# Loading, memory and order in the front part of a transformer block on one Trainium2 core

## The chip, the core and the metric

The kernel runs on one core of a Trainium2 chip. The core has a matrix engine (TensorE, "PE" in the profile), a vector engine (VectorE, DVE), a scalar engine for activations (ScalarE, ACT), a general engine (GpSimd, POOL) and a sync engine (SyncE, SP), which here issues every transfer between the chip's DRAM and the on-chip memories. Matmul results land in PSUM, a small memory of eight banks; everything else on chip lies in SBUF, 128 partitions wide. Each engine works through its own queue in order and waits on semaphores. The metric is the device time of one execution in microseconds; lower is better.

## The reference, cut to what matters

The reference is one hybrid block on x of 1024 positions by 1024 channels, all in float32. Its input projection `w_in` feeds three mixers, and the changed part of the kernel is what stands in front of their attention:

```
hn = rms_norm(x, norm_mix_g)
u  = hn @ w_in            # columns: MLA 672 | fox q,k,v,f 1544 | z, xBC, dt | gates
c_q (384), c_kv (256), k_rope (32) = split(u_mla)
q  = rms_norm(c_q) @ w_uq      # 8 heads of 96
kv = rms_norm(c_kv) @ w_ukv    # 8 heads of 64 + 64
q, k = rope_tail(rms_norm(q)), rope_tail(rms_norm(k))    # rotation by positions
fox: q, k = rms_norm per head of 64; log_f = log_sigmoid(f + b_f), cumulated
ssm: dt = softplus(dt_raw + dt_bias); cumulated dt*A; y * silu(z)
```

Behind it come two attentions (MLA and "fox", the latter with forget gates), a state-space scan, the gated merge, and a gated MLP with a short convolution.

## The kernel before, in words

All matmuls keep float32 accuracy by splitting: each operand is written as a high part (rounded to the matmul's format, `split`, L142, on ScalarE) and the remainder (L143, on VectorE). `mm3` (L167) then issues three matmuls per 128-deep slice: high by high, high by low, low by high. Activations must also be transposed on TensorE before they can be the stationary operand; a transposed group goes through PSUM and is split from there.

The tokens are eight tiles of 128. The front part has three stages.

*Latents* (L351 to L405). For each token tile: load x, `norm_tile` (square and sum on ScalarE, an inverse root by eleven or so short VectorE instructions, the scaled row, then eight transposes and the split into `hnh`, `hnl`); two products with the latent columns of `w_in`, 384 columns (`cq`) and 312 columns (`ckv`: 288 latent columns, 8 forget-gate and 16 dt columns); their normalisation into `cn`; five transposes and the split into `ch[t]`, `cl[t]`. The weights are loaded by `wsplit` through five buffers `raw`: sixteen loads of one 128-row slice each, and sixteen tiny ones for the 8 and 16 columns. `rope_and_columns` builds the cosine and sine tables with a long chain of GpSimd instructions, loads the positions so that each partition gets eight single numbers, and turns parameter rows into columns by transposes.

*Heads and values* (L422 to L519). For each tile: `q` (18 matmuls of 384 columns) and `kv` (12 of 512) from the latents, head norms, rotation on GpSimd, 16 transposes into four PSUM groups, split, and four kinds of stores to DRAM (`q_h`, `q_l`, `k_h`, `k_l`). The fox values (`fxv`, 24 matmuls of 256 columns per tile) come in two halves behind the loop over tiles, each half with weights of its own (`load_cols`) in the same buffers.

*Wide projections* (L615 to L683). Four blocks of 512 columns (z first half, fox q, fox k, z second half), eight tiles each, 24 matmuls of 512 columns per tile (`fx`). `load512` loads and splits a block's weights at its beginning, through the two `wr` buffers. The q and k units are normalised per head, transposed at once, split and stored; `gate_sums` computes the cumulated forget gates and decays between the first two blocks. `down_sums` prepares sums of the MLP's down weights on GpSimd, through four buffers `t4`.

[...] Only inside a `tc.manual_schedule(engines=...)` does the named engine keep the written order. Before the change there was none in the front part; from attention on, TensorE (and in attention VectorE too) was already in written order.

PSUM in the front: four buffers `mm` and two `mv` for results, and two `tp` for transposes, eight banks in all. SBUF is a stack of pools: a new pool may lie where a closed one lay, and its tiles wait for the last use of what was there.

Of the kernel before, what the change touches and what calls it, by code (L numbers as in the profile page):

```python
# [11 lines left out]
F32 = mybir.dt.float32  # L12
# [30 lines left out]
def block_kernel(ctx: ExitStack, tc: tile.TileContext, x, positions, norm_mix_g, w_in, b_gate,  # L43
# [132 lines left out]
    def norm_tile(pool, tag, spool, psp, xt, gbc, h, l, t, ptag):  # L176
# [12 lines left out]
        if wide:  # L189
            A.activation(xn, xg, AF.Copy, scale=r)  # L190
        else:
            V.scalar_tensor_tensor(out=xn, in0=xt, scalar=r, in1=gbc, op0=ALU.mult, op1=ALU.mult)
        half, c0 = t // 4, (t % 4) * P
# [29 lines left out]
    def rope_and_columns(rp):  # L223
# [18 lines left out]
        pos_i = rp.tile([P, NT], I32, name="pos_i", tag="pos_i", bufs=1)  # L242
        SY.dma_start(pos_i, positions.rearrange("o (t p) -> p (o t)", p=P))
        pos_f = rp.tile([P, NT], F32, name="pos_f", tag="pos_f", bufs=1)
        tc.keep_in_program_order(G.tensor_copy(pos_f, pos_i))
# [49 lines left out]
        pr = rp.tile([84, P], F32, name="pr_g", tag="pr", bufs=1)  # L295
        SY.dma_start(pr[0:24, :], b_gate.rearrange("o (r p) -> (o r) p", p=P))
        SY.dma_start(pr[24:72, :], ssm_conv_w.rearrange("o k (r p) -> (o k r) p", p=P))
        SY.dma_start(pr[72:84, :], ssm_conv_b.rearrange("o (r p) -> (o r) p", p=P))
        pt = psp.tile([P, 84], F32, name="pcp", tag="tp", bufs=2)
        T.transpose(pt, pr, ident[0:84, 0:84])  # L300
        A.activation(pc_g, pt, AF.Copy, scale=0.5)
        for dst, srcs in ((pc_f1, (ffn_conv_w[:, 0, :], ffn_conv_w[:, 1, :])),
                          (pc_f2, (ffn_conv_w[:, 2, :], ffn_conv_b))):
            pr = rp.tile([88, P], F32, name=uid("pr_f"), tag="pr", bufs=1)
            for i, s in enumerate(srcs):
                SY.dma_start(pr[44 * i:44 * i + 44, :], s.rearrange("o (r p) -> (o r) p", p=P))
            pt = psp.tile([P, 88], F32, name=uid("pcp"), tag="tp", bufs=2)
            T.transpose(pt, pr, ident[0:88, 0:88])
            A.activation(dst, pt, AF.Copy)
        pr = rp.tile([NK, P], F32, name="pr_n", tag="prn", bufs=1)  # L310
        SY.dma_start(pr, ssm_norm_g.rearrange("o (r p) -> (o r) p", p=P))
        pt = psp.tile([P, NK], F32, name="pcn", tag="tp", bufs=2)
        T.transpose(pt, pr, ident[0:NK, 0:NK])
        A.activation(pc_n, pt, AF.Copy)
# [11 lines left out]
    pmla = ExitStack()  # L326
# [5 lines left out]
    ch = [chp.tile([P, 5, P], F32R, name=f"ch{t}", tag=f"ch{t}") for t in range(NT)]  # L332
    cl = [chp.tile([P, 5, P], F32R, name=f"cl{t}", tag=f"cl{t}") for t in range(NT)]

    with ExitStack() as p0:
# [6 lines left out]
        def wsplit(pool, tag, shape, pieces):  # L342
            h = pool.tile(shape, F32R, name=tag + "h", tag=tag + "h", bufs=1)
            l = pool.tile(shape, F32R, name=tag + "l", tag=tag + "l", bufs=1)
            for k, c0, c1, srcs in pieces:
                raw = mp.tile([P, 384], F32, name=uid("raw"), tag="raw", bufs=5)
                for a, b, src in srcs:
                    SY.dma_start(raw[:, a:b], src)
# [7 lines left out]

        load_x(0)
        gmix = bcast(norm_mix_g[0], D, "gmix", ap_)
        norm_tile(ap_, "xn", mp, psp, xts[0], gmix, hnh, hnl, 0, "tp")
        load_x(1)  # L360
        w1h, w1l = wsplit(mp, "w1", [P, NK, 384], [
            (k, 0, 384, [(0, 384, w_inv[:, k, C_Q:C_Q + 384])]) for k in range(NK)])
        w2h, w2l = wsplit(mp, "w2", [P, NK, 312], [
            (k, 0, 312, [(0, 288, w_inv[:, k, C_KV:C_KV + 288]),
                         (288, 296, w_inv[:, k, C_F:C_F + 8]),
                         (296, 312, w_inv[:, k, C_DT:C_DT + 16])]) for k in range(NK)])
# [1339 lines left out]
```

## Time and profile before

| what | us |
|---|---|
| median of three runs | 2099.43 (2095.68 to 2100.97) |
| profiled execution, own time | 2103.04 |
| its span in the trace | 2101.3 |
| TensorE busy in the span | 2030.5 (97%) |
| VectorE, ScalarE, GpSimd busy | 1400.8, 953.7, 619.9 |
| span up to the last `fx` matmul | about 428 |

"Busy" is the time in which an engine had at least one instruction under way. Matmuls are pipelined, so a busy TensorE isn't one at its peak; "PEclk" is the share of its full clock that the chip granted. A wait is listed with the instruction that ended it.

### The profile page before, as it was taken

What the parts mean: (1) busy time and instruction counts of PE and PEld (TensorE: products, weight loads), DVE (VectorE), ACT (ScalarE), POOL (GpSimd) and SP (SyncE); (2) the same over time, 40 slices, a digit from 0 to 9 for tenths busy, and PEclk for the clock granted to TensorE, in tenths of its full rate; (3) what the DMA queues carried; (4) which work ended last, traced back from release to release, by engine and by line L of the source; (5) the groups of instructions that cost most, each with busy time, mean ns of one, the idle gap of its engine ahead of it and who ended that gap; (6) DMA issues with size and microseconds to landing.
All of it is one profiled execution on the core that took longest, in us unless ns stands there. A gap on an engine that the chain in (4) does not pass through costs nothing.

```text
span 2101.3 us, 29138 instructions
## 1 busy us (share of the span) xinstructions
PE 2030.5 (97%) x10265; PEld 1685.4 (80%) x10265; DVE 1400.8 (67%) x2595; ACT 953.7 (45%) x1739; POOL 619.9 (30%) x606
## 2 busy tenths in 40 slices
PE   7999898999999999999999999999989999999999
PEld 6898787788888888787777888888778888887887
DVE  5687467456667776666887346556887666765664
ACT  5555222146565666554554323223444544444432
POOL 2454122322222222220000031001454455431755
PEclk9999999999999999999999999999999999999999
DMA  5057767754443554324342665441122222229675
GB/s 172 25 178 223 230 211 238 241 154 115 124 130 95 135 150 125 95 87 138 112 136 77 200 190 191 150 141 51 61 95 85 81 80 90 81 88 350 238 222 194
DMA packets 276650, 303.62 MB, mean 144 GB/s; under 512 B 19308, under 2 KB 209784, under 8 KB 276504
## 3 DMA queue, kind: packets, MB, share of 16 engines
q1 hardware_dynamic: 276504, 301.76, 46.6%
q8 instruction: 81, 1.33, 0.3%
q14 instruction: 65, 0.53, 0.1%
HBM read 209.03 MB, written 92.67 MB: 144 GB/s over the span
## 4 chain that ended last, share of the span: by engine, by line
PE 78%; DMA 8%; DVE 6%; POOL 3%; issue 2%; ACT 2%; SPq 1%; DVEq 0%; ACTq 0%; POOLq 0%
PE mm L796 18%; PE dn L1653 9%; PE ybr L167 8%; PE ua L1322 5%; PE uc L1322 4%; PE ud L1322 4%; PE wo L1368 4%; PE s L886 4%; PE fx L167 4%; PE tp L955 2%; PE ub L1322 2%; DMA att_d<-o 2%; PE fxv L167 1%; PE o L926 1%; PE kv L167 1%
## 5 line engine op out<-in xcount | busy, mean ns | idle before, releaser
L796 PE MATMUL mm<-hnh,wh 128*128 128x512 f32 x576 | 250.6, 435 | 0.0
L796 PE MATMUL mm<-hnh,wl 128*128 128x512 f32 x576 | 227.0, 394 | 0.0
L796 PE MATMUL mm<-hnl,wh 128*128 128x512 f32 x576 | 225.6, 392 | 0.0
L908 POOL TENSOR_SCALAR pm<-pm,rs 128x128 f32<-128x128 f32 (+7 forms) x128 | 108.0, 846 | 349.9 <-DVE rs L907 316.7
L1653 PE MATMUL dn<-dr,dr 128*128 128x512 f32 x592 | 182.2, 389 | 0.0
L961 DVE TENSOR_TENSOR ptl<-tp,pth 128x512 fp32r<-128x512 f32 (+1 forms) x160 | 101.3, 633 | 86.4 <-ACT pth L960 85.6
L891 DVE TENSOR_REDUCE nmx<-s 128x1 f32<-128x128 f32 (+2 forms) x192 | 105.6, 550 | 56.1 <-PE s L889 44.5
L901 ACT ACTIVATE pm<-s,nmx 128x128 f32<-128x128 f32 (+2 forms) x192 | 109.7, 576 | 55.5 <-DVE nmx L898 38.1
L1653 PEld LDWEIGHTS dn<-dr,dr 128*128 128x128 f32 x592 | 111.1, 188 | 23.0
L796 PEld LDWEIGHTS mm<-hnh,wl 128*128 128x128 f32 x576 | 108.3, 188 | 24.8
L796 PEld LDWEIGHTS mm<-hnl,wh 128*128 128x128 f32 x576 | 109.2, 190 | 18.5 <-issue 4.1
L796 PEld LDWEIGHTS mm<-hnh,wh 128*128 128x128 f32 x576 | 109.0, 189 | 17.8 <-issue 4.1
L960 ACT ACTIVATE pth<-tp 128x512 fp32r<-128x512 f32 (+1 forms) x160 | 88.2, 551 | 70.2 <-PE tp L955 69.4
L886 PE MATMUL s<-qk,qk 96*128 96x384 f32 (+5 forms) x480 | 117.6, 350 | 1.0 <-ACT pm L901 0.9
L1238 POOL TENSOR_TENSOR mg<-mg,gl 128x512 f32<-128x512 f32 x16 | 24.9, 1560 | 315.2 <-DVE gl L1235 315.1
L1653 PE MATMUL dn<-dr 128*128 128x512 f32 x296 | 115.3, 390 | 0.3 <-ACT dX L1657 0.3
L142 ACT ACTIVATE wh<-wr 128x1024 fp32r<-128x1024 f32 (+1 forms) x47 | 43.0, 914 | 145.1 <-PE ua L1322 60.8
L167 PE MATMUL fx<-w5h,hnh 128*128 128x512 f32 x256 | 101.8, 402 | 7.1 <-ACT w5h L142 7.1
L143 DVE TENSOR_TENSOR dr<-dr,dr 128x1024 fp32r<-128x1024 f32 x52 | 73.4, 1411 | 52.5 <-ACT dr L142 47.5
L167 PE MATMUL fx<-w5h,hnl 128*128 128x512 f32 x256 | 101.3, 397 | 0.0
L167 PE MATMUL fx<-w5l,hnh 128*128 128x512 f32 x256 | 101.0, 396 | 0.0
L167 PE MATMUL ybr<-al,wh 128*128 128x512 f32 x256 | 99.2, 390 | 0.0
(469 smaller groups left out, 5822.8 us busy)
## 6 DMA issues: line engine op xcount, KB each, us to landing
dr<-act_d SPq DMA_DIRECT2D x99, 256.0 KB
wr<-in_ffn_w_up_dram SPq DMA_DIRECT2D x47, 512.0 KB
wr<-in_w_in_dram SPq DMA_DIRECT2D x36, 512.0 KB
g_d<-t SPq DMA_DIRECT2D x24, 512.0 KB
gl<-g_d SPq DMA_DIRECT2D x24, 512.0 KB
ws<-in_ffn_w_down_dram SPq DMA_DIRECT2D x22, 512.0 KB
wsum_d<-ws SPq DMA_DIRECT2D x22, 512.0 KB
act_d<-fa SPq DMA_DIRECT2D x22, 512.0 KB
```

Source lines behind the costliest of these rows:

```text
L143: return i, le.tensor_sub(l, src, f32(h))
L167: T.matmul(ps, a(k), b(k), start=(i == 0), stop=(i == n - 1))
L796: T.matmul(ps, a[:, k, :], b[half][:, k, :], start=(k == 0 and i == 0), stop=(k == NK - 1 and i == 2))
L886: T.matmul(ps[:, :w], q_[:, qs], k_[:, a:a + w], start=i_ == 0, stop=not last and i_ == len(o.passes) - 1)
L891: later(c + 0.1, lambda ps=ps, ci=ci, a=a, b=b: V.reduce_max(nmx[:, ci:ci + 1], ps[:, :b - a], axis=AX, negate=True))
L901: pss[ci][1][0] = later(c + 0.9 + 0.1 * ci, lambda ci=ci, a=a, b=b: A.activation(p_[:, a:b], pss[ci][0][:, :b - a], AF.Exp, bias=nb, accum ...
L908: G.tensor_scalar(p_[:, 0:n * P], p_[:, 0:n * P], rs[:, 3:4], 0.0, op0=ALU.mult, op1=ALU.add)
L960: later(c + 0.05, lambda th=th, pt=pt, off=off: A.activation(th[:, :off], pt[:, :off], AF.Copy))
L961: pl[0] = later(c + 0.6, lambda th=th, tl=tl, pt=pt, off=off: V.tensor_sub(tl[:, :off], pt[:, :off], f32(th[:, :off])))
L1322: T.matmul(ps, a, b, start=first and n == 0, stop=n == 11, skip_group_check=not first)
L1368: T.matmul(p, a, b, start=k == 0 and i == 0, stop=k == NK - 1 and i == 2)
L1653: T.matmul(ps[m], a[:, ts_], b[:, 512:], start=first_ and j == 0 and q == 0, stop=j == NFH - 1 and q == 2, skip_group_check=not first_)
```

## The change

Loads. The latent columns are loaded as pieces of up to three 128-row slices by 672 columns (`load_cols2`, `split_cols2`), the first six slices into memory that belongs to the later tiles `chB` and `clB`, the rest through small buffers. The 8 and 16 tiny columns come by two loads for all slices at once. Positions are loaded as 8 rows of 128, cast, transposed on TensorE and copied; the parameter rows get buffers of their own and are loaded together.

Memory. `ch` and `cl` become four tiles of four tokens each. The second half of the value weights is split into the tiles of the first four tokens (`chA`, `clA`) once these are used. The raw columns of the first z block get a pool of their own (`zr`), the later blocks use the `wh` and `wl` buffers of the later fill work, the `t4` buffers also hold `Fh` and `Fl`, and `fsh`, `fsl` get two buffers each.

Order. `norm_tile` is cut into `norm_chain` and `norm_turn`, the latent norm from its transposes. TensorE keeps the written order from the third tile's turning to the end of the values; in the wide stage TensorE, VectorE and ScalarE do. The values move into the loop over tiles, head turnings come two tiles late, fox turnings two units late, weight splits are spread over the odd units of the block before, and `gate_sums` becomes a generator in seven steps.

```diff
+        def load_cols2(k0, k1, c0=0, c1=672):
+            if k1 <= 6:
+                raw = wraw[k0 // 3][:, k0 % 3:k0 % 3 + k1 - k0, :]
...
+            SY.dma_start(raw, w_inv[:, k0:k1, C_Q + c0:C_Q + c1])
...
+        chain(0)
+        for part in parts:
+            split_cols2(*part)
+        split(w2h[:, :, 288:312], w2l[:, :, 288:312], rfd)
+        turn(0)
...
+        pe_front = tc.manual_schedule(engines={mybir.EngineType.PE})
+        pe_front.__enter__()
+        turn(2)
+        next(rot)
+        for t in range(1, NT):
+            if t + 4 < NT:
+                load_x(t + 4)
+            if t + 2 < NT:
+                chain(t + 2)
+            p1 = latent(t, 0)
+            latent_turn(t - 1)
+            p2 = latent(t, 1)
+            if t + 2 < NT:
+                turn(t + 2)
+            latent_norm(t, p1, p2)
...
+    def heads_turn(t, qn, kn):
+        for src, col, dsts in ((qn, gq_col, (q_h, q_l)), (kn, gk_col, (k_h, k_l))):
+            for g in range(2):
+                pt = tps()
+                for j in range(4):
+                    T.transpose(pt[:96, j, :], src[:, 4 * g + j, :], ident)
+                sh = mp.tile([96, 4, P], F32R, name=uid("sh"), tag="sh")
+                sl = mp.tile([96, 4, P], F32R, name=uid("sl"), tag="sl")
+                A.activation(sh, pt[:96, :, :], AF.Copy, scale=col)
+                V.scalar_tensor_tensor(out=sl, in0=pt[:96, :, :], scalar=col, in1=f32(sh),
+                                       op0=ALU.mult, op1=ALU.subtract)
...
         for t in range(NT):
+            if t > 1:
+                heads_turn(*heads.pop(0))
+            if t == 4:
+                vcols.append(load_v(*(f32r_halves(four(n)) for n in ("chA", "clA")), 256))
...
+            heads.append((t, qn, kn))
+            if t == 0:
+                latent_turn(NT - 1)
+            values(t, 0, fv_tile(False))
+            if t > 4:
+                values(t - 5, 256, fv_tile(False))
+        pup.close()
+        zrp = pup.enter_context(TP("zr", 1, side="right"))
+        load512(C_Z)
+        for n, ts in ((0, (3, 4)), (1, (5, 6, 7))):
+            heads_turn(*heads.pop(0))
+            for t in ts:
+                values(t, 256, fv_tile(True))
     pmla.close()
+    pe_front.__exit__(None, None, None)
...
+    w5 = [set512(n) for n in (1, 0)][::-1]
...
+    for _ in range(NK // 2):
+        split512()
...
+        with tc.manual_schedule(engines={mybir.EngineType.PE, mybir.EngineType.DVE, mybir.EngineType.Activation}):
+            for i, which in enumerate((3, 0, 1, 4)):
+                wh, wl = w5[i]
+                for t in range(NT):
+                    if which != 4 and t == 0:
+                        load512({3: C_FQ, 0: C_FQ + 512, 1: C_Z + 512}[which])
+                    if which != 4 and t % 2:
+                        split512()
+                    if units % 5 in (1, 3) and units // 5 * 2 + units % 5 // 2 < NFH:
+                        down_sums(units // 5 * 2 + units % 5 // 2)
+                    p = acc("fx", "mv" if units % 3 == 2 else "mm")
+                    units += 1
+                    mm3(p, tok(hnh, t), tok(hnl, t), lambda k: wh[:, k, :], lambda k: wl[:, k, :], NK)
+                    if which != 3 or t in (2, 3):
+                        next(gs, None)
+                    if waiting and waiting[0][0] <= units - 2:
+                        turned(*waiting.pop(0)[1:])
```

More of the change, by code (lines that the diff above doesn't have):

```diff
@@ L423, in load_cols, with values, load512 @@
             split(h[:, k:k + 2, :], l[:, k:k + 2, :], raw)
         return h, l
+    def values(t, c0, vt):
+        vh, vl = vcols[c0 // 256]
+        p = acc("fxv", "mv")[:, 0:256]
+        mm3(p, tok(hnh, t), tok(hnl, t), lambda k: vh[:, k, :], lambda k: vl[:, k, :], NK)
+        split(vt[:, :, 0:64], vt[:, :, 64:128], p.rearrange("p (h d) -> p h d", d=64))
+        SY.dma_start(fv_d[t * P:(t + 1) * P, c0 // 64:c0 // 64 + 4, :], f32(vt))
+    raws = []
+    def load512(c0):
+        for k in range(0, NK, 2):
+            if c0 == C_Z:
+                raw = zrp.tile([P, 2, 512], F32, name=uid("raw"), tag="zr", bufs=4)
+            else:
+                raw = f32(fpl.tile([P, 2, 512], F32R, name=uid("raw"), tag=("wh", "wl")[k // 2 % 2]))
+            SY.dma_start(raw, w_inv[:, k:k + 2, c0:c0 + 512])
+            raws.append((k, raw))
@@ L612, in gate_sums @@
         SY.dma_start(cum_d.rearrange("a r s -> r a s"), f32(ct))
[L615 to L625 removed]
+    with px:
         def down_sums(k):
```

363 lines of the change are left out of this document (188 added, 175 removed).

## The prediction

> **What bounds the kernel now.** I read the page's head, then busy time by stage, what TensorE waited for, the first instructions of each stage, the granted clock in short slices, and the chain for the pace of each matmul. The page's head:
>
> ```profile
> span 2101.3 us, 29138 instructions
> ...
> PE 2030.5 (97%) x10265; PEld 1685.4 (80%) x10265; DVE 1400.8 (67%) x2595; ACT 953.7 (45%) x1739; POOL 619.9 (30%) x606
> ```
>
> TensorE is the bound: whatever shortens its path shortens the run. Busy time in four stretches, which I call the latents, the heads, the wide projections and the rest (columns: length, busy and count for TensorE, its weight loads, VectorE, ScalarE, GpSimd; clock; DMA share; GB/s):
>
> ```profile
> 0.00:97.00 97.00, 80.59 (x482) 77.12 (x482) 59.68 (x249) 49.11 (x138) 37.63 (x93) 0.96 0.32 95
> 97.00:227.00 130.00, 113.94 (x762) 104.79 (x762) 101.50 (x267) 67.37 (x143) 53.27 (x120) 0.98 0.66 195
> 227.00:429.00 202.00, 190.67 (x857) 155.82 (x858) 116.12 (x308) 48.35 (x72) 57.51 (x44) 0.97 0.70 225
> 429.00:2101.00 1672.00, 1645.28 (x8166) 1347.63 (x8164) 1123.52 (x1773) 788.84 (x1389) 471.52 (x349) 1.00 0.44 134
> ```
>
> The rest, 1672 us, is busy for 1645 and isn't edited. The first 429 us hold 385.2 us of TensorE, so 43.8 us of idle time, and the longest waits there are these (total, times, longest):
>
> ```profile
> PE pt L198 <- DVE xn L192: 9.1, 1, 9.1
> PE tp L403 <- DVE cn L396: 7.7, 2, 4.2
> PE fx L167 <- ACT w5h L142: 7.1, 1, 7.1
> PE tp L673 <- DVE fv L665: 5.6, 1, 5.6
> PE tp L673 <- DVE fqn L669: 4.0, 3, 2.6
> ```
>
> They are 33.5 us of the 43.8. Two stage borders, by the first rows of the tiles `q` and `fx` (min/median/max ns, first and last start):
>
> ```profile
> L167 PE MATMUL q<-uqh,ch x48: 331/334/443, 97.7 to 177.0; 128*128 128x384 f32 x48
> ```
>
> ```profile
> L167 PE MATMUL fx<-w5h,hnh x256: 387/389/793, 227.7 to 427.6; 128*128 128x512 f32 x128
> ```
>
> The head stage starts at 97.7, the wide stage at 227.7; behind the last start, 427.6, come two more matmuls, so I take 428.4 as its end. Idle time also costs afterwards, by the granted clock (the column after GpSimd):
>
> ```profile
> 35.00:40.00 5.00, 1.10 (x5) 1.13 (x6) 4.25 (x36) 1.69 (x13) 0.00 (x0) 0.79 0.65 204
> 40.00:45.00 5.00, 5.00 (x19) 4.96 (x18) 4.35 (x13) 1.54 (x3) 2.37 (x1) 0.53 0.06 7
> ...
> 225.00:230.00 5.00, 2.34 (x6) 1.86 (x7) 4.53 (x11) 2.27 (x3) 0.00 (x0) 0.56 0.28 104
> 230.00:235.00 5.00, 5.00 (x19) 4.00 (x17) 1.38 (x2) 1.12 (x2) 0.00 (x0) 0.76 0.66 210
> ...
> 340.00:345.00 5.00, 1.89 (x9) 1.23 (x7) 4.29 (x8) 1.79 (x4) 2.86 (x3) 1.00 1.04 326
> ...
> 390.00:395.00 5.00, 2.39 (x14) 1.74 (x13) 4.44 (x9) 0.09 (x1) 1.96 (x2) 1.00 0.68 248
> ```
>
> In 35 to 40 TensorE stood 3.9 of the 5 us, and the clock was 0.79 there and 0.53 in the next slice; after the 7.1 us before 227.7 it was 0.56 and 0.76. Each episode lost 0.68 x 5 = 3.4 us. The 2.6 us idle in 390 to 395 lost nothing, so an idle time that cools the clock lies between 2.6 and 3.9 us.
>
> **The change part by part.** TensorE now goes in the written order from the third token on, so I add up its work in that order and then the places where the order must wait. Pace, from the chain (start, us, what, count):
>
> ```profile
> 57.33 1.57 PE ckv L167 x11
> ...
> 60.88 1.76 PE cq L167 x10
> ...
> 114.46 2.76 PE kv L167 x12
> ...
> 126.47 3.12 PE q L167 x18
> ...
> 130.81 3.60 PE fxv L167 x30
> ...
> 205.75 0.87 PE tp L500 x8
> ...
> 394.16 34.26 PE fx L167 x151
> ```
>
> Per instruction: `ckv` 0.143, `cq` 0.176, `kv` 0.230, `q` 0.173, `fxv` 0.120, a transpose 0.109, `fx` 0.227 us.
>
> *Latents.* The old order loads 16 narrow pieces of weights and 16 tiny ones; the new one issues 6 wide loads and 2 tiny-column loads.
>
> ```profile
> 0.00:20.00 20.00, 9.43 (x37) 8.01 (x37) 11.97 (x42) 9.99 (x19) 6.22 (x34) 1.00 0.82 245
> ```
>
> ```profile
> 2.18 2.73 SPq L348 DMA_DIRECT2D raw<-in_w_in_dram  x5
> ...
> 12.67 5.24 SPq L348 DMA_DIRECT2D raw<-in_w_in_dram  x9
> ...
> 20.23 10.29 SPq L348 DMA_DIRECT2D raw<-in_w_in_dram  x18
> ```
>
> Those 32 loads keep the queue's issuer until 30.5 us. The new set, two x tiles and the gain are 1024 x 696 x 4 B = 2.85 MB and 3 x 0.52 MB: 4.4 MB, 18 us at 245 GB/s. With first issue and landing I take 21 us for the last columns (18 at best; 31 if the tiny columns come as late as now). [...] Behind them lie 24 `ckv` matmuls (3.4) and the three turnings of the first tokens (24 x 0.109 = 2.6): the second token starts at 27. All latents are 192 x 0.176 + 192 x 0.143 + 104 x 0.109 = 72.5 us; 10.3 are done by then, 62.2 remain, which gives 89.2. Each latent turning is written 24 `cq` matmuls (4.2 us) and a turning (0.9) behind the matmuls it depends on; normalising took longer than that twice (7.7 us in the waits). I add 3.3, between 0 and 7.7: the head stage starts at **92.5** (86 to 106), 5.2 us earlier. On the SP queue the weights and the tiny columns now go ahead of the third x tile and the two latent gains, which are wanted only after 27; the column parameters' eight loads and the positions, a transpose and a ScalarE copy come with the rotation tables, and these run on GpSimd between the `xg` products. Their cover is ScalarE (49 of 97 us busy) and GpSimd (38 of 97); without it each late table or x tile would hold a turning for its own microsecond or two.
>
> *Heads and values.* TensorE: 144 x 0.173 + 96 x 0.230 + 384 x 0.120 + 128 x 0.109 = 25.0 + 22.1 + 46.1 + 13.9 = 107.1 us. Against the 130.0 us of now this looks like 23 us of gain; the order takes most of it back. `heads_turn` puts four groups of four transposes in a row, on two PSUM buffers, so the third group waits until ScalarE and VectorE have emptied the first. How long emptying takes (start, us):
>
> ```profile
> 205.59 1.03 PE L500 MATMUL tp<-ident,qn 128*96 128x128 f32 x8
> ```
>
> ```profile
> 206.23 1.26 ACT L503 ACTIVATE sh<-tp,gq_col 96x512 fp32r<-96x512 f32 x2 [1.21 <-PE tp L500]
> ```
>
> ```profile
> 206.94 1.41 DVE L504 SCALAR_TENSOR_TENSOR sl<-tp,gq_col,sh 96x512 fp32r<-96x512 f32 x2 [1.47 <-ACT sh L503]
> ```
>
> From 205.6 TensorE transposes two groups (0.87); VectorE has emptied the first by 207.6 and the second by 208.4. The third group could start at 207.6 instead of 206.5, and the fourth has to wait 0.4 more: 1.55 us each time, for eight tokens **12.4 us** (no less, since the two copies need their 0.63 and 0.70 after the transposes even on free engines; 24 if the groups find instructions of some 0.7 us ahead of them in both queues). Second, the token's normalisation and rotation must end before its turning, now two tokens later:
>
> ```profile
> 143.58 0.94 DVE L475 TENSOR_REDUCE ssq<-sq 128x8 f32<-128x768 f32 x1
> ```
>
> ```profile
> 155.83 0.46 POOL L448 TENSOR_TENSOR qn<-rp,rp 128x128 f32<-128x128 f32 x1
> ```
>
> From the reduction to the last rotation is 12.7 us; the cover is one token's values and the next token, 2.9 + 10.5 + 1.6 = 15.0, less ScalarE's squares and copies before the reduction: 1792 elements a row, 2.2 us by estimate at the 0.63 us per 512 of the `sh` row. That just holds; I add 4.5 (0 to 15) for VectorE's and GpSimd's order, still the planner's, and for values that stand behind the single `fv` buffer. Third, the first value weights lie where the latent weights lay and can't be loaded before:
>
> ```profile
> 104.88 0.94 SPq L422 DMA_DIRECT2D raw<-in_w_in_dram  x2
> ```
>
> ```profile
> L167 PE MATMUL fxv<-v,hnh x256: 277/283/387, 117.1 to 220.2; 128*128 128x256 f32 x128
> ```
>
> Load to first use took 12.2 us; `q` and `kv` of one token cover 5.9 plus a latent turning, so 3.5 (0 to 6). The second half in used latents' memory is asked for a whole token ahead, 13 us, and costs nothing; without cover it would be those 6 once more. Heads: 107.1 + 12.4 + 4.5 + 3.5 = 127.5, end at **220.0**, no shorter than now.
>
> *Border.* The raw columns of z are loaded under the last values; the split into the w5 buffers has to wait for the memory below, part of which holds value weights to the last matmul. One ScalarE and one VectorE piece then lie bare: 2.5 us (0 to the 7.1 of now). As that is short, the 3.4 us of lost clock go too. The wide stage starts at 222.5.
>
> *Wide projections.* 768 x 0.227 + 64 x 0.109 = 181.4, and 2.3 for the gate sums' 21 small matmuls and transposes at a transpose's pace. Now VectorE and ScalarE are also in written order. VectorE's load:
>
> ```profile
> L143 DVE TENSOR_TENSOR w5l<-raw,w5h 128x1024 fp32r<-128x1024 f32 x16 | 20.3, 1274 | 19.4 <-ACT w5h L142 19.4
> ...
> L656 DVE SCALAR_TENSOR_TENSOR zt<-th,fx 128x512 f32<-128x512 f32 x15 | 10.3, 685 | 38.4 <-ACT th L654 27.1 <-DMA z_d<-zt 11.3
> ```
>
> Of 116.1 us busy in this stage, 20.3 are weight splits and 10.3 the z units; 85.5 remain for the 16 query and key units and the gates, and 8 splits of 1.27 fall among them: 95.7, while TensorE needs 16 x 5.45 + 7.0 + 2.3 = 96.5. Level; the transposes come two units (11 us) late and six PSUM buffers lie between, which covers most. The gate logarithms move out of the head stage into z units, where VectorE has little else. `Fh` and `Fl` now take two of the four `t4` buffers, so ScalarE stands until the down-weight sums before them are through GpSimd; behind it queue `fsq` and `fsh`, and TensorE for the turning two units on. I add 4.8 (0 to 20): 188.5, end at **411.0**.
>
> **Sum.** 428.4 - 411.0 = 17.4 us less. Against the profiled execution's 2103.0 that is 2085.6; its time stands 3.6 above the median of the runs shown, 2099.4, so I predict 2082.
>
> **Rivals.**
> *All covers hold* (2063): no 3.3, 3.5, 4.5, 2.5 or 4.8, 18.6 us less. For it: none of these is a bound by busy time. Against: VectorE is level with TensorE in the last stage.
> *Transfers set the last stage* (2096): it moved 225 GB/s; were that all it can have, it stays 202 instead of 188.5 us, and 3.9 of the 17.4 are left. Against: 326 GB/s in 340 to 345. For: that slice also has a share of 1.04 and TensorE idle.
> *The turnings cool the clock* (2109, slower): eight times, 16 transposes and the wait are 1.74 + 1.55 = 3.3 us without an ordinary matmul. If the clock falls then, each costs the 3.4 us seen above, 27.2 together, 9.8 more than the gain: with six such tokens the gain is gone, with seven the kernel is measurably slower. Against: a transposing array isn't idle, and 1.55 lies under 2.6. [...]
>
> **How the numbers follow.** Forecast 0.47, all covers 0.25, transfers 0.15, cooling 0.13. About 0.3% (6.3 us) is what can be told from no change. The forecast itself reaches from 2070 to 2095. Faster: 0.42 + 0.25 + 0.02 = 0.69. Same: 0.05 + 0.12 + 0.01 = 0.18. Slower: 0.01 + 0.12 = 0.13. The range goes from 2056, 7 below the case with all covers, as the first columns may land 3 us sooner and the unedited rest may move a few, to 2106, which leaves out most of the cooling.
>
> **What would show it.** `q` first at about 92 and `fx` at about 222; TensorE waiting for `sl` in `heads_turn` some 1.5 us per token; no clock under 0.9 after 50 us; `fx` ending near 411 with a rest of 1672. I am wrong if the head stage is near 110 us, or if VectorE or DMA waits stand in it instead; and if the rest changes by more than 5 us, which this sum holds fixed though the planner places its ScalarE, GpSimd and DMA work anew.

## The result, and the profile after

The changed kernel takes 2115.0 us (median of four runs, 2112.2 to 2119.4) where the kernel before takes 2098.7 beside it: a ratio of 1.0081, 95% interval 1.0063 to 1.0098. It is 0.8% slower, where 2082 had been forecast. The profiled execution took 2116.95 us. The busy times on its page:

```profile
PE 2038.6 (96%) x10266; PEld 1692.3 (80%) x10266; DVE 1403.6 (66%) x2586; ACT 952.5 (45%) x1731; POOL 621.6 (29%) x606
```

TensorE is busy 8 us longer than before with as many matmuls (10266 against 10265 in the traces); some of them were slower, as the clock below shows. Busy time in the four stretches, cut where the first `q`, the first `fx` and the end of `fx` lie (columns as before):

```profile
0.00:106.60 106.60, 83.10 (x488) 78.38 (x489) 65.70 (x253) 53.55 (x140) 39.74 (x103) 0.95 0.33 103
106.60:246.80 140.20, 120.53 (x760) 110.27 (x758) 90.42 (x235) 62.63 (x130) 49.58 (x110) 0.94 0.56 175
246.80:438.20 191.40, 186.99 (x854) 153.92 (x855) 126.78 (x326) 47.73 (x74) 58.10 (x44) 0.99 0.73 233
438.20:2115.00 1676.80, 1647.95 (x8168) 1349.70 (x8166) 1120.66 (x1773) 788.58 (x1389) 474.17 (x349) 1.00 0.43 133
```

The latents now take 106.6 us instead of 97.7, the heads and values 140.2 instead of 130.0, the wide projections 191.4 instead of 200.7, the rest 1676.8. So the wide stage gave about what was forecast, and both stages ahead of it lost. The two borders:

```profile
L167 PE MATMUL q<-uqh,chA x24: 334/334/522, 106.6 to 150.7; 128*128 128x384 f32 x24
```

```profile
L167 PE MATMUL fx<-w5h,hnh x256: 387/389/628, 246.8 to 437.3; 128*128 128x512 f32 x128
```

What TensorE waited for up to 450 us:

```profile
PE tp L518 <- DVE sl L522: 11.1, 9, 1.8
PE pt L201 <- DVE xn L192: 10.6, 1, 10.6
PE tp L433 <- DVE cn L424: 4.8, 4, 2.4
PE pcn L258 <- DVE r L159: 2.7, 1, 2.7
PE tp L518 <- POOL qn L543: 2.5, 1, 2.5
...
PE fxv L167 <- ACT vh L142: 2.3, 2, 1.2
PE cq L167 <- DVE w1l L143: 2.1, 2, 1.9
PE fxv L167 <- DVE vl L143: 1.7, 4, 0.6
PE fx L167 <- ACT w5h L142: 1.4, 1, 1.4
...
PE pt L201 <- ACT xn L190: 1.3, 1, 1.3
```

Of the old waits the first x tile's 9.1 us are 10.6 now, the 7.7 for `cn` are 4.8, the border's 7.1 are 1.4 (`w5h`), and the 5.6 for `fv` are gone. In their place stand 11.1 us in nine waits for `sl` inside `heads_turn`, and several waits at the head of the written order: ahead of the positions' transpose (`pcn`), for norms (`cn`, `xn`) and for rotated heads (`qn`). And the clock falls more often in the head stage. In the kernel before it fell there once, and a window over most of the stage behind that has it whole:

```profile
105.00:110.00 5.00, 3.66 (x12) 2.98 (x13) 2.80 (x8) 1.48 (x5) 1.77 (x9) 0.66 0.44 132
...
115.00:220.00 105.00, 99.96 (x699) 93.29 (x698) 82.57 (x218) 54.13 (x109) 50.66 (x107) 1.00 0.74 215
```

In the changed kernel seven slices of 5 us are below it, the first at the end of the latents and six in the head stage:

```profile
100.00:105.00 5.00, 3.96 (x18) 3.99 (x19) 2.14 (x7) 0.81 (x2) 2.11 (x10) 0.66 0.41 113
...
120.00:125.00 5.00, 4.55 (x19) 4.36 (x20) 4.03 (x11) 1.01 (x2) 2.55 (x5) 0.66 0.40 107
...
170.00:175.00 5.00, 2.01 (x11) 1.55 (x12) 3.61 (x13) 1.57 (x3) 2.06 (x6) 0.78 0.45 169
175.00:180.00 5.00, 5.00 (x20) 4.80 (x19) 3.63 (x8) 1.86 (x3) 3.95 (x9) 0.54 0.77 216
...
190.00:195.00 5.00, 3.17 (x18) 2.67 (x16) 2.87 (x5) 2.68 (x5) 4.76 (x14) 0.83 0.65 195
195.00:200.00 5.00, 5.00 (x23) 4.65 (x23) 1.70 (x3) 2.14 (x5) 0.87 (x2) 0.83 0.60 172
...
210.00:215.00 5.00, 4.98 (x22) 4.88 (x22) 1.46 (x3) 1.85 (x3) 2.44 (x6) 0.66 0.84 254
```

### The profile page after: what moved, and what is told of

The parts are those of the page before. It is cut to its first block, busy times and chain, and to the rows that moved or that the text cites. A ratio compares the mean times of both kernels' runs of the same rounds, so it can differ in the third digit from the quotient of the medians.

```text
span 2115.2 us, 29040 instructions
## 1 busy us (share of the span) xinstructions
PE 2038.6 (96%) x10266; PEld 1692.3 (80%) x10266; DVE 1403.6 (66%) x2586; ACT 952.5 (45%) x1731; POOL 621.6 (29%) x606
## 4 chain that ended last, share of the span: by engine, by line
PE 82%; DVE 7%; DMA 4%; ACT 2%; issue 2%; POOL 1%; SPq 1%; DVEq 0%; ACTq 0%; POOLq 0%
PE mm L918 17%; PE dn L1775 10%; PE ybr L167 8%; PE fx L167 6%; PE ua L1444 5%; PE uc L1444 4%; PE ud L1444 4%; PE wo L1490 4%; PE s L1008 4%; PE tp L1077 3%; PE ub L1444 2%; DMA att_d<-o 2%; PE fxv L167 1%; PE q L167 1%; PE o L1048 1%
```

## The experiments

For each kernel I read the same three numbers: the first start of `q`, the first start of `fx` and the last start of `fx`, from the rows of these tiles (the end of `fx` is about 0.8 us behind its last start). "Heads" is the second less the first; "wide" the third less the second plus 0.8. All in us; the ratio is to runs of the kernel before on the same chip.

| kernel | first `q` | heads | wide | last `fx` | span | median | ratio, 95% interval |
|---|---|---|---|---|---|---|---|
| before | 97.7 | 130.0 | 200.7 | 427.6 | 2101.3 | 2098.7 | |
| after | 106.6 | 140.2 | 191.3 | 437.3 | 2115.2 | 2115.0 | 1.0081 (1.0063 to 1.0098) |
| e1, written order in the wide stage only | 95.3 | 118.2 | 194.3 | 407.0 | 2081.2 | 2083.6 | 0.9926 (0.9902 to 0.9950) |
| e4, in heads and wide | 95.6 | 140.1 | 192.7 | 427.6 | 2102.0 | 2103.9 | 1.0021 (1.0010 to 1.0033) |
| e3, in latents and heads | 107.2 | 142.5 | 187.7 | 436.6 | 2110.0 | 2112.6 | 1.0063 (1.0043 to 1.0083) |
| e5, nowhere | 95.6 | 119.1 | 185.9 | 399.8 | 2075.9 | 2077.4 | 0.9892 (0.9872 to 0.9912) |
| e2, head turning in halves | 108.4 | 126.8 | 192.1 | 426.5 | 2100.8 | 2101.8 | 1.0003 (0.9994 to 1.0013) |
| e7, waits filled with matmuls | 108.4 | 135.7 | 189.3 | 432.6 | 2108.0 | 2109.9 | 1.0053 (1.0036 to 1.0070) |
| e6, two latent steps later | 108.0 | 140.2 | 192.3 | 439.7 | 2114.5 | 2112.5 | 1.0066 (1.0047 to 1.0085) |
| e9 = e5, weights late | 96.7 | 119.2 | 186.6 | 401.7 | 2076.1 | 2076.0 | 0.9891 (0.9874 to 0.9907) |
| e10 = e5, single `fsh`, `fsl` | 95.5 | 118.4 | 192.5 | 405.6 | 2077.2 | 2079.7 | 0.9906 (0.9886 to 0.9927) |
| e13 = e5, two raw buffers | 95.4 | 117.0 | 188.0 | 399.6 | 2075.6 | 2080.4 | 0.9908 (0.9886 to 0.9930) |
| e12 = e5, values behind the loop | 96.8 | 115.0 | 188.4 | 399.4 | 2071.6 | 2074.4 | 0.9880 (0.9859 to 0.9901) |
| e11 = e12, old value memory | 95.5 | 118.1 | 190.0 | 402.8 | 2080.9 | 2081.8 | 0.9913 (0.9888 to 0.9938) |
| e14 = e12, both old buffers | 96.7 | 113.2 | 194.1 | 403.2 | 2074.2 | 2080.9 | 0.9901 (0.9875 to 0.9927) |
| e15 = e12, z columns late | 95.3 | 122.7 | 187.5 | 404.7 | 2080.2 | 2080.8 | 0.9899 (0.9873 to 0.9925) |

What lies behind the last `fx` + 0.8, which no kernel edits, took from 1670.2 (e14) to 1677.3 us (e11), 1672.9 before and 1677.1 after. So a few us of a whole time are not the edit's, and I rest verdicts on stages first.

### Where the written order stands

My theory after the result was that the written order on TensorE is what costs (A); its rival, that the new loads or the shared memory do (B). Where no written order holds, the compiler's planner orders an engine's instructions: in the kernel before, `fxv`, written behind the loop over tokens, started at 117.1 us, while `q` of that loop went on to 177.0.

e1 takes TensorE's written order away ahead of the wide stage:

```diff
-        pe_front = tc.manual_schedule(engines={mybir.EngineType.PE})
-        pe_front.__enter__()
...
-    pe_front.__exit__(None, None, None)
```

> TensorE's written order is kept in the wide stage alone; in latents and heads the planner orders TensorE again, with the new loads and the new memory. Theory A (the written order in latents and heads is what costs: two PSUM buffers in `heads_turn`, late norms in the latents, the clock that falls behind 16 transposes and a wait): `q` starts at 92 to 98, `fx` at 226 to 232 instead of 246.8, the wide stage stays at about 191 us, the whole is 2093 to 2101. Rival B (the new loads or the shared memory cost, whatever the order): `q` still at about 106, `fx` at 243 or later, the whole within 4 us of the changed kernel's 2115.

A, and more than it asked: `fx` starts at 213.5, 33.3 us earlier than in the changed kernel, with the same loads and memory, and the kernel is faster than the one before.

e4 lets it begin with the heads:

```diff
-        pe_front = tc.manual_schedule(engines={mybir.EngineType.PE})
-        pe_front.__enter__()
         turn(2)
         next(rot)
...
+        pe_front = tc.manual_schedule(engines={mybir.EngineType.PE})
+        pe_front.__enter__()
         for t in range(NT):
             if t > 1:
                 heads_turn(*heads.pop(0))
```

> TensorE's written order begins only with the loop over heads and values; the planner orders the latents. A: if the order costs in the latents too, `q` starts at 92 to 98 instead of 106.6 and the head stage still takes about 140 us, so the whole is about 2104 to 2108. B (the loads set the latents): `q` at about 106 again, the whole 2112 to 2118.

A: `q` starts at 95.6 and the head stage takes 140.1 us as in the change; the whole, 2103.9, lies at the lower edge of its range. The order in the latents costs 106.6 - 95.6 = 11.0 us, the one in the heads 140.1 - 118.2 = 21.9.

e3 takes it away in the wide stage alone:

```diff
-        with tc.manual_schedule(engines={mybir.EngineType.PE, mybir.EngineType.DVE, mybir.EngineType.Activation}):
+        with ExitStack():
```

> The wide stage goes back to the planner (TensorE, VectorE and ScalarE), latents and heads stay in written order. A: the wide stage's 9 us of gain come from its order, so it takes 199 to 203 us again and the whole is 2121 to 2127. B: the gain there comes from the earlier weights and the double `fsh`, `fsl` buffers, so the stage stays at 190 to 193 us and the whole at 2112 to 2118.

Here A failed. Without its order the wide stage isn't 200 us but 187.7, below B's range too, and the stage's gain must be in loads and buffers. Part of it is paid at the border: TensorE stood 3.7 us ahead of the first `fx` instead of 1.4 in the changed kernel.

e5 makes both edits, e1's and e3's.

> No written order anywhere in the front: the new loads and the new memory alone, all engines ordered by the planner. From the two kernels that have one half of it (the front by the planner: `q` at 95.3, `fx` at 213.5; the wide stage by the planner: 187.8 us behind a border of 4 us) the sum is `fx` at 214 to 217, a wide stage of 188 to 194, and 2077 to 2086 for the whole: the written order in the wide stage is then worth nothing, and all of the change's gain is its loads and memory. Rival: the written order does earn something in the wide stage, where the kernel with a planned wide stage had only a late start to thank for its short one; then the wide stage is 196 to 201 and the whole 2087 to 2095.

The sum of the halves holds, with a wide stage 2 us below its range. With no written order the change is 1.1% faster than the kernel before, and in the wide stage the listing has no wait of TensorE but the border's, 2.4 us for `w5h`. Against e1 the order in the wide stage costs 194.3 - 185.9 = 8.4 us of that stage, and 6.2 of the whole, where the two intervals just overlap; behind a written front (after against e3) it is 0.7 by the last `fx`. Nowhere did it earn anything.

### What the order costs in the heads

e2 cuts `heads_turn` in two halves, `qn` ahead of the token's `q` matmuls and `kn` between these and `kv` (behind the loop, between `values`):

```diff
         for src, col, dsts in ((qn, gq_col, (q_h, q_l)), (kn, gk_col, (k_h, k_l))):
+            if src is kn:
+                yield
...
-            if t > 1:
-                heads_turn(*heads.pop(0))
+            ht = heads_turn(*heads.pop(0)) if t > 1 else iter(())
+            next(ht, None)
...
                 A.activation(qn[:, 4 * i:4 * i + 4, :], p[:, :384].rearrange("p (h d) -> p h d", d=96), AF.Copy)
+            next(ht, None)
```

> Everything in written order as in the change, but the 16 transposes of a head turning are parted: the eight of `qn` before the `q` matmuls, the eight of `kn` between `q` and `kv`. A: TensorE's waits for `sl` (11.1 us) go, and no token has over 2.5 us without an ordinary matmul in a turning, so the clock stays up (about 5 us): the head stage takes 124 to 131 us instead of 140.2 and the whole is 2099 to 2106. Rival: GpSimd's and VectorE's chain per token sets the pace of the stage, the freed time turns into waits for `qn` or `fv`, the stage stays above 136 us and the whole at 2111 or more.

```profile
PE tp L520 <- POOL qn L545: 4.9, 2, 4.1
...
PE tp L520 <- DVE sl L524: 1.2, 1, 1.2
```

The wait for `sl` fell from 11.1 to 1.2 us, the stage to 126.8. So four transposed groups in a row on two PSUM buffers cost 13.4 us, with what they did to the clock. But a part of the freed time went the way of the rival: `qn`, from GpSimd, is now waited for 4.9 us, once for 4.1.

How much of the 13.4 is the wait, and how much the clock? e7 keeps the wait and fills the pause with eleven matmuls whose result nothing reads.

`warm` is the accumulator of the token's first `q`, whose real matmuls overwrite it:

```diff
                 pt = tps()
+                if warm is not None and src is kn:
+                    for _ in range(7 - 3 * g):
+                        T.matmul(warm[:, :384], ch[NT - 1][:, 0, :], uqh[:, 0, 0:384], start=True, stop=True)
```

> The change as it is, but in the six head turnings inside the loop eleven extra matmuls (7 ahead of the third group of transposes, 4 ahead of the fourth; `uqh` by a latent, into the accumulator that the token's first real `q` matmul overwrites) fill the waits for `sl`. They add 1.9 us of work per token where the waits are 1.1 to 1.8 us. Cooling theory (transposes and waits leave the array without ordinary matmuls, 3.9 us of that halve the clock): the `q` matmuls behind the turnings near 172, 189 and 207 us go at 0.17 us each instead of 0.32, which saves 4.8 us, the extra work costs 6 x 0.1 to 0.8: head stage 136 to 138 instead of 140.2. Rival (the slow matmuls come from something else, such as their operands or the pure wait): they stay at about 0.32 us and the stage is 140 to 144.

The same turning in both, by the timeline of TensorE (start, length). In the changed kernel:

```profile
189.42 1.03 PE L518 MATMUL tp<-ident,qn 128*96 128x128 f32 x8
192.27 1.44 PE L518 MATMUL tp<-ident,kn 128*96 128x128 f32 x8 [1.81 <-DVE sl L522]
193.36 0.67 PE L167 MATMUL q<-uqh,chB 128*128 128x384 f32 x1
193.83 0.52 PE L167 MATMUL q<-uql,chB 128*128 128x384 f32 x1
194.15 0.52 PE L167 MATMUL q<-uqh,clB 128*128 128x384 f32 x1
```

With the pause filled:

```profile
189.00 1.04 PE L521 MATMUL tp<-ident,qn 128*96 128x128 f32 x8
189.79 1.47 PE L519 MATMUL q<-uqh,chB 128*128 128x384 f32 x7
191.85 0.64 PE L521 MATMUL tp<-ident,kn 128*96 128x128 f32 x4 [0.58 <-DVE sl L525]
192.25 0.94 PE L519 MATMUL q<-uqh,chB 128*128 128x384 f32 x4
...
193.38 0.42 PE L167 MATMUL q<-uqh,chB 128*128 128x384 f32 x1
```

In both the last transposes give way to `q` at 193.4. Without ordinary matmuls from 189.4 to 193.4 the first ten `q` start about 0.32 us apart; with them, 0.17. The same holds near 172 and 207 us, and the clock of these slices is whole again (1.00 in e7 from 170 to 180, from 190 to 200 and from 210 to 215):

```profile
175.00:180.00 5.00, 5.00 (x33) 4.74 (x33) 4.82 (x10) 2.34 (x4) 2.77 (x5) 1.00 0.75 213
```

The stage is 140.2 - 135.7 = 4.5 us shorter although the extra work is done, so the cooling in these turnings costs at least that (6.8 us by the slices). By the 4.5, about 9 of e2's 13.4 are the wait; the split is rough, as e2 has a pause of its own, the 4.1 us for `qn`. e7 shows that these turnings lower the clock as long as the pause is empty. That the 16 transposes count with it is my reading and not shown, since the pause of 1.81 us alone was never run. For it speaks a pause with no transpose in it, 1.69 us at 200.95 in the kernel before, which left the clock whole (1.00, inside the window shown above). Against it speaks the border of the changed kernel: 1.42 us and, one matmul later, 0.76 us of waiting, again with no transpose, and behind them `fx` matmuls 0.43 us apart instead of 0.23.

### What the order costs in the latents

```diff
         turn(2)
-        next(rot)
...
             p1 = latent(t, 0)
-            latent_turn(t - 1)
+            if t == 1:
+                next(rot)
             p2 = latent(t, 1)
+            latent_turn(t - 1)
             if t + 2 < NT:
                 turn(t + 2)
```

> The change with two steps moved in TensorE's written order of the latents: the transpose of the positions comes behind the second token's `cq` (it waited 2.7 us ahead of them), and each latent turning behind the `ckv` matmuls instead of ahead of them, so its norm has 3.7 us more. Theory: late inputs at the head of TensorE's order cost the latents 2.7 for the positions, 1.5 and 2.4 for `cn`, and the clock that falls at the first of them: `q` starts at 99 to 102 instead of 106.6 and the whole is 2107 to 2111. Rival (it is the coarse order itself, whole blocks of 24 matmuls, that leaves no work to fill in): `q` still at 105 or later, the whole 2113 to 2118.

```profile
PE pt L201 <- DVE clA L435: 6.8, 4, 2.4
```

A miss: the wait ahead of the positions is gone and that for `cn` is 0.8, but `q` starts at 108.0 (the latents of e2 and e7, which don't edit them, end at 108.4, so some 2 us there are not an edit's). The latent turning now stands right ahead of the next token's, which needs the same two PSUM buffers and waits 6.8 us for VectorE to empty them (`clA`).

The same two buffers are behind the wait that e6 took away. In the changed kernel the positions weren't late: GpSimd had cast them by 22.8.

```profile
22.52 0.28 POOL L256 CAST pos_c<-pos_i 8x128 f32<-8x128 int32 x1 [2.03 <-DMA pos_i<-in_positions_dram]
```

Their transpose needs a `tp` buffer, and `turn(2)` ahead of it had just filled both. VectorE emptied the first at 32.4, and the transpose followed:

```profile
31.76 0.68 DVE L205 TENSOR_TENSOR hnl<-pt,hnh 128x512 fp32r<-128x512 f32 x1
```

```profile
32.59 0.19 PE L258 MATMUL pcn<-ident,pos_c 8*128 8x8 f32 x1 [2.70 <-DVE r L159]
```

The releaser that the profile names, `r`, ended a moment later on the same engine, but the transpose doesn't read it. The column parameters' transposes stood for the same buffers, 1.2 us for `hnl` and 0.3 twice for ScalarE's copies.

Moving single steps moves the wait. What the planner does instead is seen in e4's timeline: it cuts tokens into pieces, blocks of 2 to 10 matmuls of one product with two to four transposes here and there, and between 48 and 73 us TensorE has no idle time of 0.05 us or more. That this fine mixing is the whole 11 us is not shown; a written order as fine wasn't run.

### Where the gain comes from

All following kernels have no written order; each undoes one part of the loads and memory.

e9 loads and splits at the beginning of the block:

```diff
-                    if which != 4 and t == 0:
-                        load512({3: C_FQ, 0: C_FQ + 512, 1: C_Z + 512}[which])
-                    if which != 4 and t % 2:
-                        split512()
+                if which != 3:
+                    load512({0: C_FQ, 1: C_FQ + 512, 4: C_Z + 512}[which])
+                    for _ in range(NK // 2):
+                        split512()
```

> All by the planner as in the kernel without any written order, and the weights of the three later wide blocks are loaded and split at the beginning of their own block, as before the change, instead of being spread over the block before. Theory (the 9 us of gain in the wide stage come from weights that are there early): the wide stage takes 196 to 203 us, 7 to 10 more than without this edit, and the whole 2086 to 2093. Rival (the planner moves loads and splits early by itself, and the gain comes from the double `fsh`, `fsl` buffers or the shorter border): the stage stays within 2 us and the whole at 2077 to 2086.

The rival: 186.6 us. Where a load stands in the program does next to nothing here (0.7 us); I take it that the planner brings it forward into free memory. So memory had to be taken away:

```diff
-            sh = xp.tile([P, 4, P], F32R, name=uid("fsh"), tag="fsh", bufs=2)
-            sl = xp.tile([P, 4, P], F32R, name=uid("fsl"), tag="fsl", bufs=2)
+            sh = xp.tile([P, 4, P], F32R, name=uid("fsh"), tag="fsh", bufs=1)
+            sl = xp.tile([P, 4, P], F32R, name=uid("fsl"), tag="fsl", bufs=1)
```

> The kernel without any written order, with one buffer each for `fsh` and `fsl` again instead of two. Theory: in the kernel before, ScalarE stood 37 us of the wide stage until a store had taken the old `fsh` away, and that is what made norms and turnings late there (5.6 and 4.0 us of TensorE waiting); with one buffer these waits come back, the wide stage takes 190 to 197 us instead of 186 and the whole is 2081 to 2088. Rival: the stage's gain comes from the weights' memory (ScalarE stood 27 us for `raw` before); then it stays within 2 us of 186 and the whole at 2074 to 2080.

e13 is e9 with two raw buffers instead of four, each split following its load:

```diff
-                raw = f32(fpl.tile([P, 2, 512], F32R, name=uid("raw"), tag=("wh", "wl")[k // 2 % 2]))
+                raw = f32(fpl.tile([P, 2, 512], F32R, name=uid("raw"), tag="wh"))
...
+            if c0 != C_Z:
+                split512()
```

> The kernel without any written order, with the weights of the three later wide blocks loaded and split at the beginning of their own block and through two raw buffers instead of four, as in the kernel before. Theory of the weights' memory: ScalarE stands some 27 us for `raw` again and the wide stage takes 190 to 197 us instead of 186, the whole 2081 to 2088. Rival (the double `fsh`, `fsl` are the gain): within 2 us of 186, the whole 2074 to 2080.

ScalarE's waits in the wide stage, in the kernel before:

```profile
ACT w5h L142 <- DMA raw<-in_w_in_dram: 26.9, 10, 7.5
ACT fsh L677 <- DMA fk_h<-fsh: 21.9, 5, 6.5
ACT fsh L677 <- DMA fq_h<-fsh: 15.1, 4, 5.2
```

with the single `fsh`:

```profile
ACT fsh L758 <- DMA fk_h<-fsh: 26.6, 4, 8.6
...
ACT fsh L758 <- DMA fq_h<-fsh: 9.1, 4, 4.6
```

and with two raw buffers:

```profile
ACT w5h L142 <- DMA raw<-in_w_in_dram: 21.1, 8, 7.2
```

Both old waits came back in size (35.7 us against 37, and 21.1 against 27). The first costs the stage 6.6 us and puts the last `fx` 5.8 later; the second costs 2.1 and nothing by the last `fx`, though ScalarE stands so long in it. So the stage bears out e10's theory and not e13's. By the whole time neither is told apart from e5 (the intervals overlap). e14 makes both edits on e12, which stands below:

> The fastest kernel so far (no written order, second values behind the loop, 2074.4) with both undone at once: one buffer each for `fsh` and `fsl`, and the later wide blocks' weights at the beginning of their block through two raw buffers. Theory: the two waits on ScalarE (37 us for stores and 27 us for `raw` in the kernel before) add up in one queue, so the wide stage takes 196 to 201 us as before the change (188.4 without this edit), the whole 2082 to 2088. Rival: alone they cost 6.5 and 2 us and no more together, or hide each other: 192 to 196, the whole 2077 to 2082; what is left of the old 200.7 is then the border's.

The rival again: 194.1 us, 5.7 more than e12, less than the two alone together. 200.7 - 194.1 = 6.6 us of the old wide stage stay unexplained.

e12 writes the second half of the values behind the loop again:

```diff
-            if t > 4:
-                values(t - 5, 256, fv_tile(False))
...
-        for n, ts in ((0, (3, 4)), (1, (5, 6, 7))):
+        for n, ts in ((0, (0, 1, 2, 3)), (1, (4, 5, 6, 7))):
```

> The kernel without any written order, with the second half of the values written behind the loop over tokens again; its weights still go into `chA`, `clA` at the fifth token. Theory: under the planner the place in the program does not matter as long as the memory is free, so `q` to `fx` takes 118 to 121 us as with the values inside the loop (119.1), the whole 2074 to 2081. Rival: the place sets the planner's choice and the stage takes 123 or more, the whole 2081 or more.

e11 is e12 with the second half's weights in the first half's buffers:

```diff
-            if t == 4:
-                vcols.append(load_v(*(f32r_halves(four(n)) for n in ("chA", "clA")), 256))
...
+        vcols.append(load_v(*(fvp.tile([P, NK, 256], F32R, name=uid(n), tag=n) for n in ("vh", "vl")), 256))
```

> As the kernel with the second half of the values behind the loop, and its weights go into the buffers of the first half again, so that they can be split only when the first half's last matmul is through. Theory: that wait, which stood among the 4 us of waits for values between 186 and 202 in the kernel before, is what the used latents' memory removes: `q` to `fx` takes 122 to 127 us instead of 119, the whole 2080 to 2087. Rival: head turnings left over cover the load, the stage stays at 118 to 121 and the whole at 2074 to 2081.

e15 is e12 with z's raw columns in the memory of the later blocks', free only behind the last values:

```diff
...
-        load512(C_Z)
         for n, ts in ((0, (0, 1, 2, 3)), (1, (4, 5, 6, 7))):
...
-    for _ in range(NK // 2):
-        split512()
     pup.close()
     pfl = ctx.enter_context(ExitStack())
     fpl = pfl.enter_context(TP("fill", 2, side="right"))
+    load512(C_Z)
+    for _ in range(NK // 2):
+        split512()
```

> The fastest kernel so far with the raw columns of the first wide block loaded late: no pool of their own, they go where the later blocks' go, in memory that is free only when the last values' stores are through. Theory: the border (2.6 us from the last value to the first `fx`) is 7 us or more again, the clock falls behind it, and `fx` starts at 216 to 220 instead of 211.8; the whole 2079 to 2085. Rival: the split for the first block must wait for memory below anyway, so the border grows by under 2 us and the whole stays at 2072 to 2078.

```profile
PE fx L167 <- ACT w5h L142: 9.5, 1, 9.5
```

The late z columns are clear in the stage: a border of 9.5 us instead of 2.6, `fx` at 218.0 instead of 211.8 and its end 5.3 us later; by the ratios of the whole time e15 and e12 can't be told apart. For the value memory the stage (118.1 against 115.0) lies in the rival's range and the whole, 7.4 us longer, in the theory's, but of the 9.3 us between the two profiled executions 5.9 lie behind the last `fx`, and the stage moved by 1.8 in e14 too, where nothing in it was edited. So its part is not shown. Values behind the loop didn't cost, and e12, the fastest, at 0.988 of before, can't be told from e5 by its interval.

## Why the prediction was wrong

The sum against the profiled execution: 14.1 us too little for the latents, 11.2 for heads and values (138.7 from 106.6 to the last value's end at 245.3, against 127.5), 1.1 too much for the border, 2.9 too little for the wide stage, 4.1 for the rest. Together 31.2, which leads from 2085.6 to the 2117 of the profiled execution.

*Latents: 92.5 forecast, 106.6 measured.* The step that failed is "Their cover is ScalarE (49 of 97 us busy) and GpSimd (38 of 97)": what the written order puts between the products was priced at nothing. An idle ScalarE or GpSimd doesn't cover it where a transpose needs a PSUM buffer that VectorE has yet to empty, and in written order TensorE can't go round it. The forecast counted the two `tp` buffers in the heads and not here. The second token starts at 32.7 instead of 27: TensorE stood 2.7 us ahead of the positions and 1.3 for `xn`, and the clock took 1.7 (0.76 and 0.90 in the slices from 20 to 30). The other 8.4 us lie behind that: late `cn` 4.8 (2.4 of it the last) where the sum had 3.3, the column parameters' transposes 1.8, and the clock 1.7 (0.79 and 0.87 from 30 to 40) and 1.7 at 100 to 105; 1.7 us stay open. With the planner the same loads give 95.6, so 11.0 us of the miss are the order's and 3 stand without it.

The term ahead of these, last columns at 21, came out by luck. ScalarE split the last of them without having waited, so they were there by 16.5:

```profile
16.46 0.35 ACT L142 ACTIVATE w2h<-rfd 128x192 fp32r<-128x192 f32 x1
```

```profile
5.00:15.00 10.00, 4.43 (x16) 3.96 (x17) 8.07 (x28) 6.83 (x13) 0.00 (x0) 1.00 1.02 348
```

The loads moved 348 GB/s from 5 to 15 us, where the forecast took 245. TensorE went on only at 21 because it waited 1.9 us for a split on VectorE (`w1l`), which took 2.72 us beside a GpSimd instruction (last section).

*Heads: 127.5 forecast, 138.7 measured.* The waits came in size: 11.1 for `sl` against 12.4, 2.5 for `qn` against 4.5, 4.0 for the value weights (`vh` and `vl`) against 3.5; with TensorE's work of 107.1 that is 124.7. Not in the sum, which was made from paces at full clock, was the clock. By the prediction's own method the six slices from 120 us on lost 5 x (0.34 + 0.22 + 0.46 + 0.17 + 0.17 + 0.34) = 8.5 us. The first of them, 1.7 us, stands behind the waits for the value weights, and the kernel before has such a slice too (105 to 110); the other 6.8 stand behind turnings. (5.5 us more stand in short pieces that I can't name one by one.) The step that failed is the rival's "Against", "a transposing array isn't idle, and 1.55 lies under 2.6": the pause had to be taken with the transposes around it, 3.9 us, if the reading of e7 above is right. The rival's mechanism was right, at a chance of 0.13, and its price too large: three of the six turnings inside the loop cooled (near 172 behind 2.5 us for `qn` as well), 6.8 us by their slices and 4.5 by e7, where it had 27 for eight.

*Border and wide stage: 2.5 and 188.5 forecast, 1.4 and 191.4 measured.* Near in size, wrong in reason; the clock, held whole in the sum, fell once more behind the border (0.79 from 245 to 250). The forecast read the order as what frees TensorE of VectorE and ScalarE; e3 and e5 show 187.7 and 185.9 without it. What helps is the double `fsh` (about 6 us, e10) and, at the border, the early z columns (about 6, e15).

*The rest* was held fixed and came 4.1 longer, within the spread of kernels that don't edit it.

*The rivals.* The covers didn't all hold, and transfers didn't set the last stage: it took 191.4 us at 233 GB/s, and 185.9 in e5. The rival that was missing is the planner with the same loads. The change has two halves, of which one earned about 22 us (e5) and the other lost 38 (after against e5); the forecast added up TensorE's work in written order and credited the whole difference to both.

## What to carry to other kernels

Where a change frees memory and fixes an order at once, run the halves apart: here loads and memory were worth 1.1% and the order cost 1.8%. The order written by hand in coarse blocks turned late inputs and full PSUM buffers into pauses of TensorE, and moving one step moved the pause to the next buffer; the planner, which mixes small pieces, had none of 0.05 us or more from 48 to 73 us in e4. Behind a row of 16 transposes with 1.8 us of waiting in it `q` matmuls came 0.32 us apart instead of 0.17 in two turnings here (189 and 207 us), and with ordinary matmuls in the wait 0.17; so part such a row.

## What was not expected of the hardware

In these traces no single length of pause decides whether the clock falls. The 3.9 us from 189.4 to 193.4 did, by ten matmuls at half speed; a stretch of 4.0 us of the same kind near 157 us did not (155 to 165 is at 1.00). Behind eight transposes and 1.9 us of idle time, together 3.0 us from 18.0 to 21.0, the clock was 0.76 from 20 to 25:

```profile
20.00:25.00 5.00, 3.97 (x15) 3.33 (x16) 3.82 (x11) 1.77 (x5) 0.77 (x2) 0.76 0.26 85
...
155.00:165.00 10.00, 8.10 (x56) 7.42 (x55) 8.06 (x24) 6.06 (x13) 0.60 (x1) 1.00 0.76 233
```

And in e12 a pause of 2.48 us between ordinary matmuls, with no transpose in it, was followed within a microsecond by `kv` matmuls 0.43 us apart instead of 0.23:

```profile
102.93 0.47 PE L167 MATMUL kv<-ukh,chA 128*128 128x512 f32 x1 [2.48 <-DVE cn L424]
```

So the forecast's bounds for a cooling idle time, 2.6 to 3.9 us, don't hold. What decides beside the length, these runs don't show.

In the kernel before, three of VectorE's small operations, which take 0.17 us elsewhere in the same chain, took 1.1 to 1.2 us beside GpSimd's subtractions. VectorE:

```profile
342.05 0.17 DVE L157 TENSOR_TENSOR rs_t<-fr 128x8 f32<-128x8 f32 x1
342.25 1.12 DVE L158 TENSOR_TENSOR rs_t<-rs_t,rs_v 128x8 f32<-128x8 f32 x1
```

GpSimd at the same time:

```profile
342.06 1.28 POOL L634 TENSOR_TENSOR ws<-ws,ws 128x512 f32<-128x512 f32 x1 [3.33 <-DMA ws<-in_ffn_w_down_dram]
```

Two more follow at 343.40 (1.19 us) and 344.82 (1.13), and each long one ends as a subtraction ends: at 343.37, 344.59 and 345.95, the subtractions at 343.34, 344.56 and 345.92. By an estimate (three times 1.15 - 0.17) that made the longest wait of the old wide stage, 5.6 us ahead of the transposes at 347.5, longer by about 3 us. In the changed kernel the split that TensorE waited for near 20 us looks alike. It took 2.72 us, where one of the same shape at 21.20 took 0.55:

```profile
18.19 2.72 DVE L143 TENSOR_TENSOR w1l<-raw,w1h 128x384 fp32r<-128x384 f32 x1
```

```profile
18.07 2.42 POOL L181 TENSOR_TENSOR xg<-xt,gmix 128x1024 f32<-128x1024 f32 x1 [13.61 <-DMA xt<-in_x_dram]
```

That the GpSimd instruction held VectorE up is my reading of these times; no run here varied it.
